# State-space mixer: groups without padding on array halves, a real part in two summands, and the first gated blocks multiplied unsplit inside the loop

## The chip, the cores and the metric

The program runs on one core of a Trainium2 chip. The metric is the device time of one execution in microseconds, the median over runs. One execution was also taken by the hardware profiler; all rows below come from it. Its engines are called PE (TensorE's products), PEld (TensorE's weight loads), DVE (VectorE), ACT (ScalarE), POOL (GpSimd) and SP (SyncE, which here only issues transfers).

## The reference

A small network on 256 tokens of width 1024: six layers, each a mixer and a gated feed-forward block. The change is in the second layer's mixer, a state-space layer (S5) with 64 groups of 16 channels and 64 complex states per group, run forwards and backwards in time:

```python
def _s5_direction(u, lam_re, lam_im, log_dt, b_re, b_im, c_re, c_im, reverse):
    lam_bar = jnp.exp(lam * dt)
    b_bar = ((lam_bar - 1.0) / lam)[..., None] * lax.complex(b_re, b_im)
    bu = einsum('bsgp,gnp->bsgn', u, b_bar)          # complex
    _, hs = lax.associative_scan(combine, (a, bu), axis=1, reverse=reverse)
    return jnp.einsum('gpn,bsgn->bsgp', c, hs).real

def s5_mixer(h, ..., d_skip, w_glu):
    u = h.reshape(b, s, 64, 16)
    y = (y_fwd + y_bwd).reshape(b, s, d) + d_skip * h
    g = jax.nn.gelu(y)
    val, gate = jnp.split(g @ w_glu, 2, axis=-1)      # w_glu: 1024 x 2048
    return val * jax.nn.sigmoid(gate)
```

## The kernel before

Activations lie transposed: 8 channel tiles of 128 partitions by 256 tokens. Time is cut into chunks of L = 4 tokens, so a scan runs over NC = 64 chunk steps. A channel tile kt holds 8 groups, worked on as 4 pairs (pi) of two groups (g2), two directions (d), real and imaginary (i).

Precise products are made by splitting: a weight piece of 1024 columns (half of a 1 MB transfer `raw`, three buffers) is rounded into `whi` on ACT (L134) and the rest subtracted into `wlo` on DVE (L136); an activation is split alike (`split`, L166); three products, hi by hi, lo by hi and hi by lo, replace one float32 product. `piece(n)` (L142) keeps four pieces prepared ahead, and `hold` names the piece ahead of which preparation stops. A product on plain float32 operands appears in the trace as two records for one instruction of the program.

The mixer is `s5` (L1758). `load(kt)` fetches the tables, copies the decay `at` on ACT and scales the inputs by the norm's factor into `u` (L1805), two operations of 64 partitions; u and the output weights `wz` are padded with zeros in the other group's half (memset by POOL, L1793), so that a product of all 128 rows yields one group. `states(kt)`: 32 products into `vp` (PSUM pool `mm`, 4 banks), L1819; four DVE products from PSUM (L1823, L1824, L1826, L1827), a sum and a difference on POOL (L1825, L1828), two DVE scans (L1830, L1831), and the turn back: two products and a sum on POOL (imaginary part, L1834 to L1836), two products and a difference on DVE (real part, L1837 to L1839). `outputs(kt)`: 40 products into one bank `yp` (pool `ms`, 4 banks): a direct term from `mt` (L1849) and four state terms (L1855) for each of eight groups, all in PSUM partitions 0 to 63; a copy `ys` on ACT (L1858), two stores on SP's queue to DRAM (L1860) and one load `g` in another order on ACT's queue (L1862). `gates(kt)`: gelu on ACT (L1867) and the split into `ghi`, `glo`.

The loop (L1877) runs n = 0 to 11: states(n), gates(n - 4), load(n + 1), outputs(n - 2). Behind it, in program order, come the first half of the gated matrix (L1895, pieces 0 to 7 by channel tile, 8 blocks of 128 columns in 4 banks `pf`) and its second half (L1902, pieces 8 to 15, `blockT`), with sigmoid, product and residual per pair of blocks. In front of `s5` stands the first feed-forward block, which stages the mixer's inputs through DRAM (`s5hx`, `s5u`).

The order on each engine's queue is not written out by hand: a planner places every instruction by priority (program order) and its own estimate of when inputs and buffers are ready; the queues then run in that fixed order. `issue_after` adds an order by hand: the first gated pieces may only follow the sixth load of wz (L1888 to L1891).

## Time and profile before

| | us |
|---|---|
| median of 3 runs | 2419.71 |
| lowest and highest run | 2417.47, 2421.77 |
| the profiled execution | 2417.63 |
| its span, first to last instruction | 2415.9 |
| PE busy, share of the span | 2219.3, 92% |
| DVE busy | 1655.8, 69% |
| ACT busy | 1132.0, 47% |
| POOL busy | 628.1, 26% |

Busy is the union of an engine's instructions, its share that of the span. PE's products are pipelined: one record lasts longer than the step to the next, so costs below are read from start to start. A trace can lack a few per cent of its PE records. The mean granted clock of TensorE was 0.953 of full speed.

### The profile page before, as it was taken

The page shows a single profiled execution, that of the slowest core. Times are in us where ns is not written, and L with a number is a line of the kernel's source. Part 1 is how long each engine was busy: PE and PEld are TensorE (multiplying, and loading weights), DVE is VectorE, ACT ScalarE, POOL GpSimd, SP SyncE. Part 2 cuts the span into 40 slices and gives each one's busy share as a digit, 9 for nine tenths or more (in the row PEclk, how much of TensorE's full clock was granted, in tenths as well). Part 3 has the DMA queues.
Part 4 walks back from the last instruction along what each step waited for, and adds up shares of the span by engine and source line. Part 5 has one row for each costly group of instructions (what it writes and reads, how often), then busy time and mean ns, then how long its engine had stood idle before and what let it go on. Part 6 is the DMA issues. An engine that isn't in the chain of part 4 may idle for free.

```text
span 2415.9 us, 45760 instructions
## 1 busy us (share of the span) xinstructions
PE 2219.3 (92%) x19028; PEld 2144.8 (89%) x19028; DVE 1655.8 (69%) x2502; ACT 1132.0 (47%) x2012; POOL 628.1 (26%) x583
## 2 busy tenths in 40 slices
PE   7778786799999996999999999989999999999998
PEld 7777786799999985689999999978899899899998
DVE  7899969776656768356656665874765679467664
ACT  5334321354435565354445444754544565364442
POOL 3986746300013222010011001530200359112001
PEclk9989888999999998999999999999999999799999
DMA  4457666555564432235553554443455333434552
GB/s 167 169 181 247 221 185 168 186 189 180 190 208 153 143 140 86 72 110 184 189 178 106 189 180 174 150 146 106 158 189 180 140 122 123 110 108 148 188 180 104
DMA packets 95117, 383.41 MB, mean 159 GB/s; under 512 B 37132, under 2 KB 44956, under 8 KB 54845
## 3 DMA queue, kind: packets, MB, share of 16 engines
q1 hardware_dynamic: 72400, 359.95, 43.0%
q10 hardware_dynamic: 22508, 20.54, 3.0%
q8 instruction: 149, 2.44, 0.4%
q14 instruction: 60, 0.48, 0.1%
HBM read 361.81 MB, written 18.65 MB: 157 GB/s over the span
## 4 chain that ended last, share of the span: by engine, by line
PE 71%; DVE 15%; POOL 5%; issue 3%; DMA 3%; ACT 3%; ACTq 1%; SPq 0%; POOLq 0%; DVEq 0%
PE pg L162 8%; PE pg L164 8%; PE pg L163 8%; PE po L163 7%; PE po L164 7%; PE po L162 7%; DVE wlo L136 3%; PE f L412 1%; PE pq L162 1%; PE pk L162 1%; PE pq L163 1%; PE pq L164 1%; PE pk L163 1%; PE pk L164 1%; DMA mt<-s5ker 1%
## 5 line engine op out<-in xcount | busy, mean ns | idle before, releaser
L136 DVE TENSOR_TENSOR wlo<-raw,whi 128x1024 fp32r<-128x1024 f32 x623 | 798.7, 1285 | 412.0 <-ACT whi L134 410.7
L134 ACT CAST whi<-raw 128x1024 fp32r<-128x1024 f32 x625 | 651.1, 1047 | 668.0 <-PE pg L163 291.8
L164 PE MATMUL pg<-hhi,wlo 128*128 128x256 f32 x1920 | 545.4, 284 | 24.2 <-DVE wlo L136 24.0
L162 PE MATMUL pg<-hhi,whi 128*128 128x256 f32 x1920 | 544.1, 283 | 6.8 <-ACT whi L134 6.7
L163 PE MATMUL pg<-hlo,whi 128*128 128x256 f32 x1920 | 543.2, 283 | 0.0
L164 PEld LDWEIGHTS pg<-hhi,wlo 128*128 128x128 f32 x1920 | 365.9, 191 | 27.5 <-DVE wlo L136 26.9
L162 PEld LDWEIGHTS pg<-hhi,whi 128*128 128x128 f32 x1920 | 366.2, 191 | 7.5 <-ACT whi L134 7.2
L163 PEld LDWEIGHTS pg<-hlo,whi 128*128 128x128 f32 x1920 | 366.2, 191 | 0.0
L163 PE MATMUL po<-alo,whi 128*128 128x256 f32 x1056 | 299.0, 283 | 1.6 <-DVE alo L171 1.6
L162 PE MATMUL po<-ahi,whi 128*128 128x256 f32 x1056 | 298.0, 283 | 2.2 <-ACT ahi L170 2.2
L164 PE MATMUL po<-ahi,wlo 128*128 128x256 f32 x1056 | 298.9, 283 | 0.0
L226 POOL TENSOR_TENSOR acc<-sq 128x256 f32<-128x256 f32 x16 | 15.7, 983 | 984.4 <-ACT sq L221 984.4
L162 PEld LDWEIGHTS po<-ahi,whi 128*128 128x128 f32 x1056 | 200.2, 190 | 2.4 <-ACT ahi L170 2.4
L163 PEld LDWEIGHTS po<-alo,whi 128*128 128x128 f32 x1056 | 200.5, 190 | 1.8 <-DVE alo L171 1.8
L164 PEld LDWEIGHTS po<-ahi,wlo 128*128 128x128 f32 x1056 | 200.6, 190 | 0.3 <-issue 0.2
L226 POOL TENSOR_TENSOR acc<-acc,sq 128x256 f32<-128x256 f32 x76 | 71.0, 934 | 246.4 <-ACT sq L221 228.9
L313 DVE TENSOR_TENSOR g<-pg,rB 128x512 f32<-128x512 f32 x120 | 82.8, 690 | 30.4 <-PE pg L164 30.4
L170 ACT CAST ahi<-g 128x256 fp32r<-128x256 f32 x132 | 52.5, 400 | 54.8 <-DVE g L316 54.8
L316 DVE TENSOR_TENSOR g<-g 128x256 f32<-128x256 f32 x132 | 71.8, 546 | 8.1 <-ACT g L315 8.1
L315 ACT ACTIVATE g<-g 128x256 f32<-128x256 f32 x132 | 54.2, 413 | 48.4 <-DVE g L313 34.7
L171 DVE TENSOR_TENSOR alo<-g,ahi 128x256 fp32r<-128x256 f32 x132 | 68.0, 517 | 0.0
L163 PE MATMUL pc<-hlo,whi 128*128 128x256 f32 x224 | 65.5, 292 | 0.0
(672 smaller groups left out, 5426.7 us busy)
## 6 DMA issues: line engine op xcount, KB each, us to landing
raw<-in_gu_dram SPq DMA_DIRECT2D x132, 1024.0 KB, 4.9
raw<-in_dn_dram SPq DMA_DIRECT2D x66, 1024.0 KB, 4.8
raw<-in_qkv_dram SPq DMA_DIRECT2D x36, 1024.0 KB, 4.9
raw<-in_hy_in_dram SPq DMA_DIRECT2D x13, 1024.0 KB, 4.9
raw<-in_fnet_dram SPq DMA_DIRECT2D x8, 1024.0 KB, 5.3
raw<-in_s_glu_dram SPq DMA_DIRECT2D x8, 1024.0 KB, 5.1
raw<-in_hy_out_dram SPq DMA_DIRECT2D x8, 1024.0 KB, 4.9
raw<-in_gdn_v_dram SPq DMA_DIRECT2D x8, 1024.0 KB, 4.8
```

The costliest lines, as they stand in the source:

```text
L134: nc.scalar.copy(hi[:, :w], raw[:, s:s + w])
L136: eng.tensor_tensor(lo[:, :w], raw[:, s:s + w], hi[:, :w].bitcast(F32), op=ALU.subtract)
L162: nc.tensor.matmul(ps, whi[:, sl], hi, start=start, stop=False)
L163: nc.tensor.matmul(ps, whi[:, sl], lo, start=False, stop=False)
L164: nc.tensor.matmul(ps, wlo[:, sl], hi, start=False, stop=stop)
L170: nc.scalar.copy(hi, src)
L171: nc.vector.tensor_tensor(lo, src, hi.bitcast(F32), op=ALU.subtract)
L226: nc.gpsimd.tensor_tensor(acc, sums[0], sq, op=ALU.add)
L313: nc.vector.tensor_tensor(gu_, ps, self.rB.unsqueeze(1).to_broadcast([P, 2, T]), op=ALU.mult)
L315: nc.scalar.activation(g, g, AF.Silu)
L316: nc.vector.tensor_tensor(u, u, g, op=ALU.mult)
L412: nc.tensor.matmul(o, a[:, t, c], w[:, r, :], start=n == 0, stop=n == 11)
```

## The change

Four things, all in the state-space mixer and the helper that prepares weight pieces:

- no padding: u is scaled in place (`u0`, one operation of 128 partitions), `wz` has one half less, the memsets of both go, and every product takes only its group's 64 rows, so products lie on quarters of the array (rows by group, columns by group in `states` and by pair in `outputs`). `vp` moves to the pool `ms`; `yp` becomes two banks, `ys` two copies of 128 partitions, and four stores replace two.
- the real part of the states is not subtracted: both summands stay (`s[0]`, `s[1]`) and go into the outputs as two products with the same weights; outputs have 56 products instead of 40.
- the first 8 pieces of the gated matrix are not split (`direct`): the float32 raw weights multiply the float32 gelu output `gf`, one product instead of three, inside the loop, right behind gelu. The splits of `gf` for the second half stand behind the loop.
- `hold` stands behind these 8 pieces, so their transfers may run ahead of the mixer; the order by hand at n == 6 goes.

The optional arguments `full`, `whole` and `hf` are used by no call.

```diff
+        if n in self.direct:
+            self.prep[n] = (raw[:, s:s + w], None)
+            return
...
-            wz = [sp.tile([P, 2, TW], F32, name=f"wz{i}") for i in range(2)]
+            wz = [sp.tile([P, TW], F32, name=f"wz{i}") for i in range(2)]
             def load_w(kt):
-                for g2 in range(2):
-                    r = slice(64 * g2, 64 * g2 + 64)
-                    last = nc.sync.dma_start(wz[kt % 2][r, g2], self.tab[kt, r, :TW])
-                return last.ins
+                nc.sync.dma_start(wz[kt % 2], self.tab[kt, :, :TW])
...
-            for g2 in range(2):
-                r = slice(64 * (1 - g2), 64 * (1 - g2) + 64)
-                for a in u + wz:
-                    nc.gpsimd.memset(a[r, g2], 0.0)
...
-                for g2 in range(2):
-                    r = slice(64 * g2, 64 * g2 + 64)
-                    nc.vector.tensor_tensor(u[kt % 4][r, g2], self.u0[r, 4 * kt:4 * kt + 4, :],
-                                            rc[r].to_broadcast([64, 4, NC]), op=ALU.mult)
+                u = self.u0[:, 4 * kt:4 * kt + 4, :]
+                nc.vector.tensor_tensor(u, u, rc.to_broadcast([P, 4, NC]), op=ALU.mult)
...
             def states(kt, vt, er):
-                vp = [self.mm.tile([P, 512], F32, tag="mm", name="vp") for _ in range(2)]
+                vp = [self.ms.tile([P, 512], F32, tag="ms", name="vp") for _ in range(2)]
-                            for g2 in range(2):
-                                uu = u[kt % 4][:, g2, pi, :] if d == 0 else u[kt % 4][:, g2, pi, ::-1]
+                            for r in (lo, hi):
+                                uu = self.u0[r, 4 * kt + pi, :] if d == 0 else self.u0[r, 4 * kt + pi, ::-1]
-                                nc.tensor.matmul(vp[i][64 * g2:64 * g2 + 64, sg:sg + NC], vt[:, pi, d, i, :], uu,
-                                                 start=True, stop=True)
+                                nc.tensor.matmul(vp[i][r, sg:sg + NC], vt[r, pi, d, i, :], uu, start=True, stop=True)
-                nc.vector.tensor_tensor(t[2], vp[1], er, op=ALU.mult)
-                nc.vector.tensor_tensor(t[3], vp[0], ei, op=ALU.mult)
+                nc.vector.tensor_tensor(t[2], vp[0], ei, op=ALU.mult)
+                nc.vector.tensor_tensor(t[3], vp[1], er, op=ALU.mult)
...
+                s = [x[:, :, 1:] for x in st[kt % 3]]
+                v = [x.rearrange("p (a c) -> p a c", a=8) for x in (*c, er, ei, t[1], t[3])]
+                nc.gpsimd.tensor_tensor(v[4], v[0], v[3], op=ALU.mult)
+                nc.vector.tensor_tensor(s[0], v[0], v[2], op=ALU.mult)
+                nc.gpsimd.tensor_tensor(v[5], v[1], v[2], op=ALU.mult)
+                nc.vector.tensor_tensor(s[1], v[1], v[3], op=ALU.mult)
+                nc.gpsimd.tensor_tensor(s[2], v[4], v[5], op=ALU.subtract)
-                nc.gpsimd.tensor_tensor(t[1], c[0], ei, op=ALU.mult)
-                nc.gpsimd.tensor_tensor(t[3], c[1], er, op=ALU.mult)
-                nc.gpsimd.tensor_tensor(s[1][:, :, 1:], v[1], v[3], op=ALU.add)
-                nc.vector.tensor_tensor(t[0], c[0], er, op=ALU.mult)
-                nc.vector.tensor_tensor(t[2], c[1], ei, op=ALU.mult)
-                nc.vector.tensor_tensor(s[0][:, :, 1:], v[0], v[2], op=ALU.subtract)
...
             def outputs(kt):
-                yp = self.ms.tile([P, 512], F32, tag="ms", name="yp")
-                        nc.tensor.matmul(o, mt[:, 4 * kt + pi, :], u[kt % 4][:, g2, pi, :], start=n == 0, stop=False)
-                                nc.tensor.matmul(o, w5[:, g2, pi, d, i, :], x, start=False, stop=n == 32)
+                yp = [self.ms.tile([P, 512], F32, tag="ms", name="yp") for _ in range(2)]
+                for p2 in range(2):
+                    for n in range(7):
+                        for g2 in range(2):
+                            for ph in range(2):
+                                r, pi = (lo, hi)[g2], 2 * p2 + ph
+                                if n == 0:
+                                    w, x = mt[r, 4 * kt + pi, :], self.u0[r, 4 * kt + pi, :]
+                                else:
+                                    d, i = (n - 1) // 3, (n - 1) % 3
+                                    x = s[i][r, 2 * pi + d]
+                                    x = x[:, 0:NC] if d == 0 else x[:, NC - 1::-1]
+                                    w = w5[r, pi, d, i // 2, :]
+                                nc.tensor.matmul(yp[g2][(lo, hi)[ph], p2 * NC:(p2 + 1) * NC], w, x,
+                                                 start=n == 0 and p2 == 0, stop=n == 6 and p2 == 1)
-                nc.scalar.copy(ys.rearrange("p g a c -> p (g a c)"), yp[0:64, :])
-                for g2 in range(2):
-                    nc.sync.dma_start(yx[kt, :, g2].rearrange("a q i c -> (q i) a c"), ys[:, g2])
+                for g2 in range(2):
+                    nc.scalar.copy(ys[:, g2].rearrange("p a c -> p (a c)"), yp[g2][:, :2 * NC])
+                for ph in range(2):
+                    for g2 in range(2):
+                        nc.sync.dma_start(yx[kt, ph::2, g2].rearrange("a q i c -> (q i) a c"), ys[(lo, hi)[ph], g2])
...
-            def gates(kt, g):
-                h = ss.tile([P, T], F32, tag="h", name="gl")
-                nc.scalar.activation(h.rearrange("p (c i) -> p i c", i=L), g, AF.Gelu_apprx_tanh)
-                self.split(ghi[:, kt, :], glo[:, kt, :], h)
+            first = [self.mm.tile([P, 2, T], F32, tag="mm", name="pf") for _ in range(4)]
+            def gates(k, g):
+                nc.scalar.activation(gf[:, k, :].rearrange("p (c i) -> p i c", i=L), g, AF.Gelu_apprx_tanh)
+                w, _ = self.piece(base + k)
+                for b in range(KD):
+                    nc.tensor.matmul(first[b // 2][:, b % 2], w[:, b * P:(b + 1) * P], gf[:, k, :],
+                                     start=k == 0 and b % 2 == 0, stop=k == KD - 1 and b % 2 == 1)
...
                 if 1 <= n < KD:
-                    last = load_w(n)
-                if n == 6:
-                    self.hold = None
-                    with tc.issue_after(last):
-                        self.piece(base)
+                    load_w(n)
+            for k in range(KD):
+                self.split(ghi[:, k, :], glo[:, k, :], gf[:, k, :])
+            self.hold = None
...
-            first = [self.mm.tile([P, 2, T], F32, tag="mm", name="pf") for _ in range(4)]
-            for k in range(KD):
-                whi, wlo = self.piece(base + k)
-                for b in range(KD):
...
+                    K.direct = {st["s5_glu"] + k for k in range(KD)}
...
-                K.hold = st["s5_glu"]
+                K.hold = st["s5_glu"] + KD
```

## Rows read from the trace of the kernel before

**Rows 1.** Stretches in us: length, busy PE, PEld, DVE, ACT, POOL (records), clock, DMA share, GB/s.

```profile
340.00:348.20 8.20, 8.11 (x69) 7.91 (x67) 0.80 (x3) 0.42 (x1) 0.74 (x1) 1.00 0.00 0
...
371.20:443.80 72.60, 49.02 (x883) 47.85 (x884) 66.99 (x67) 15.44 (x24) 45.00 (x31) 0.83 0.63 184
443.80:457.00 13.20, 9.58 (x104) 9.11 (x102) 13.17 (x10) 2.60 (x4) 6.79 (x4) 0.95 0.42 124
457.00:461.70 4.70, 4.70 (x79) 4.63 (x79) 1.41 (x2) 0.00 (x0) 0.00 (x0) 1.00 0.73 255
461.70:480.00 18.30, 18.03 (x152) 17.83 (x151) 8.72 (x10) 11.29 (x17) 0.00 (x0) 1.00 0.49 174
480.00:502.00 22.00, 21.80 (x192) 21.80 (x193) 19.16 (x29) 14.77 (x27) 5.14 (x6) 1.00 0.53 181
```

**Rows 2.** The chain that ended last, in order of time: start, us, what.

```profile
354.54 21.40 DMA mt<-s5ker
```

**Rows 3.** VectorE in order of time: start, us, line, operation, output<-inputs [idle before].

```profile
360.96 2.27 DVE L1830 TENSOR_TENSOR_SCAN c<-at,t 128x512 f32<-128x512 f32 x1 [0.78 <-POOL t L1825]
363.26 0.69 DVE L1837 TENSOR_TENSOR t<-c,s5ve 128x512 f32<-128x512 f32 x1
363.87 2.29 DVE L1831 TENSOR_TENSOR_SCAN c<-at,t 128x512 f32<-128x512 f32 x1
...
367.52 0.68 DVE L1827 TENSOR_TENSOR t<-vp,er 128x512 f32<-128x512 f32 x1
...
371.15 2.27 DVE L1830 TENSOR_TENSOR_SCAN c<-at,t 128x512 f32<-128x512 f32 x1 [1.15 <-POOL t L1825]
...
400.41 1.23 DVE L1831 TENSOR_TENSOR_SCAN c<-at,t 128x512 f32<-128x512 f32 x1
```

**Rows 4.** GpSimd in order of time, in the loop's first tile.

```profile
368.10 1.27 POOL L1836 TENSOR_TENSOR st<-t,t 128x512 f32<-128x512 f32 x1
```

**Rows 5.** VectorE in order of time: scalings of u, and the last tile's first scan.

```profile
352.38 3.56 DVE L1805 TENSOR_TENSOR u<-s5u,rc 64x256 f32<-64x256 f32 x8 [0.23 <-DVE rc L1781]
...
397.99 0.39 DVE L1805 TENSOR_TENSOR u<-s5u,rc 64x256 f32<-64x256 f32 x1
...
443.80 2.27 DVE L1830 TENSOR_TENSOR_SCAN c<-at,t 128x512 f32<-128x512 f32 x1 [0.80 <-POOL t L1825]
```

**Rows 6.** TensorE in order of time, records merged (xcount), in and behind the mixer.

```profile
354.19 3.67 PE L1819 MATMUL vp<-u,s5ve 128*64 128x64 f32 x60 [0.73 <-DVE u L1805]
...
391.09 2.03 PE L1819 MATMUL vp<-u,s5ve 128*64 128x64 f32 x63
...
418.84 1.11 PE L1855 MATMUL yp<-st,wz 128*64 128x64 f32 x8 [5.12 <-DVE st L1839]
...
1000.47 0.33 PE L735 MATMUL ptb<-ident,p 64*64 64x64 f32 x4
1000.74 0.33 PE L737 MATMUL ptb<-ident,p 128*128 128x128 f32 x1
...
2112.94 0.59 PE L1407 MATMUL sp<-vf,kn 128*128 128x256 f32 x2
2113.37 0.38 PE L1398 MATMUL yp<-vn,ym 128*128 128x128 f32 x2
```

**Rows 7.** Costs by line and shape in 352.4 to 457.0 us: busy, mean ns | idle before.

```profile
L136 DVE TENSOR_TENSOR wlo<-raw,whi 128x1024 fp32r<-128x1024 f32 x4 | 6.9, 1752 | 0.0
```

**Rows 8.** ScalarE in order of time: the first gelu, and the last tile's copy and gelu.

```profile
400.29 0.69 ACT L1867 ACTIVATE gl<-g 128x256 f32<-128x256 f32 x1 [4.93 <-DMA g<-yx]
400.77 0.64 ACT L1858 COPY ys<-yp 64x512 f32<-64x512 f32 x1
...
461.79 0.58 ACT L1858 COPY ys<-yp 64x512 f32<-64x512 f32 x1 [8.66 <-PE yp L1855]
...
470.35 0.66 ACT L1867 ACTIVATE gl<-g 128x256 f32<-128x256 f32 x1 [3.52 <-DMA g<-yx]
```

**Rows 9.** Costs of TensorE by line and shape over the whole span: busy, mean ns.

```profile
L735 PE MATMUL ptb<-ident,p 64*64 64x64 f32 x128 | 11.9, 243 | 0.0
```

More of the change, by code (lines that the diff above doesn't have):

```diff
@@ L69, in __init__ @@
         self.pool_lo = set()
+        self.direct = set()
+        self.hf = None
     def setup(self, rawb=3, prepb=4):
@@ L148, in piece, with blockT, rows, unitT @@
         return self.prep[n]
-    def blockT(self, base, b, KT, hi, lo, ps, u0=None):
-        hi = hi if isinstance(hi, list) else [hi[:, k, :] for k in range(KT)]
-        lo = lo if isinstance(lo, list) else [lo[:, k, :] for k in range(KT)]
+    def blockT(self, base, b, KT, hi, lo, ps, u0=None, full=None):
+        def rows(v):
+            return v if isinstance(v, list) else [v[:, k, :] for k in range(KT)]
+        hi, lo, full = (rows(v) if v is not None else [None] * KT for v in (hi, lo, full))
         for k in range(KT):
-            self.unitT(base, (b * KT if u0 is None else u0) + k, hi[k], lo[k], ps, k == 0, k == KT - 1)
-    def unitT(self, base, u, hi, lo, ps, start, stop):
+            self.unitT(base, (b * KT if u0 is None else u0) + k, hi[k], lo[k], ps, k == 0, k == KT - 1, full[k])
+    def unitT(self, base, u, hi, lo, ps, start, stop, full=None):
         nc = self.nc
@@ L161, in unitT @@
         sl = slice(c, c + P)
+        if wlo is None:
+            nc.tensor.matmul(ps, whi[:, sl], full, start=start, stop=stop)
+            return
         nc.tensor.matmul(ps, whi[:, sl], hi, start=start, stop=False)
@@ L214, in norm_block @@
             self.split(self.hhi[:, k, :], self.hlo[:, k, :], xk, self.gains[:, self.gi, k:k + 1])
+            if self.hf is not None:
+                self.nc.scalar.activation(self.hf[:, k, :], xk, AF.Copy, scale=self.gains[:, self.gi, k:k + 1])
         self.square(self.sums, xk, k == KD - 1)
@@ L292, in sin_turn, with ffn @@
         nc.scalar.activation(out, out, AF.Sin)
-    def ffn(self, gu, dn, next_gi, post=None, full=False, side=(), each=None):
+    def ffn(self, gu, dn, next_gi, post=None, full=False, side=(), each=None, whole=None):
         nc, hp = self.nc, self.hp
         with self.tc.tile_pool(name="ffn", bufs=1, reuse_waits="tile") as fp, self.tc.tile_pool(name="ffs", bufs=2, reuse_waits="tile") as fs:
-            ahi = fp.tile([P, KF, T], F32R, name="ahi")
-            alo = fp.tile([P, KF, T], F32R, name="alo")
+            if whole is None:
+                ahi = fp.tile([P, KF, T], F32R, name="ahi")
+                alo = fp.tile([P, KF, T], F32R, name="alo")
+                af = None
+            else:
+                ahi = alo = None
+                af = fp.tile([P, KF, T], F32, name="af")
             first = [self.mm.tile([P, 2, T], F32, tag="mm", name="pf") for _ in range(2)]
@@ L308, in ffn @@
                     if 2 * j + i >= 3:
-                        self.blockT(gu, 2 * j + i, KD, self.hhi, self.hlo, ps[:, i])
+                        self.blockT(gu, 2 * j + i, KD, self.hhi, self.hlo, ps[:, i], full=whole)
                 if j == 0:
@@ L315, in ffn, with out_proj @@
                 nc.scalar.activation(g, g, AF.Silu)
-                nc.vector.tensor_tensor(u, u, g, op=ALU.mult)
-                self.split(ahi[:, j, :], alo[:, j, :], u)
+                if whole is None:
+                    nc.vector.tensor_tensor(u, u, g, op=ALU.mult)
+                    self.split(ahi[:, j, :], alo[:, j, :], u)
+                else:
+                    nc.vector.tensor_tensor(af[:, j, :], u, g, op=ALU.mult)
             for _ in side:
                 pass
-            self.out_proj(dn, KF, ahi, alo, next_gi, post, lambda: fp.tile([P, KD, T], F32, name="m"), full, each)
-    def out_proj(self, base, KT, hi, lo, next_gi, post=None, mtile=None, full=False, each=None, nk=0):
+            self.out_proj(dn, KF, ahi, alo, next_gi, post, lambda: fp.tile([P, KD, T], F32, name="m"), full, each, whole=af)
+    def out_proj(self, base, KT, hi, lo, next_gi, post=None, mtile=None, full=False, each=None, nk=0, whole=None):
         nc, hp = self.nc, self.hp
@@ L339, in out_proj @@
                 ps = self.mm.tile([P, 512], F32, tag="mm", name="po")[:, :T]
-                self.blockT(base, b, KT, hi, lo, ps)
+                self.blockT(base, b, KT, hi, lo, ps, full=whole)
             if post is None:
@@ L1782, in s5 @@
             at = [sp.tile([P, 8, NC], F32, name=f"at{i}") for i in range(2)]
[L1783 to L1785 removed]
+            st = [[sp.tile([P, 8, NC + 1], F32, name=f"st{i}{j}") for j in range(3)] for i in range(3)]
             mt = sp.tile([P, NP, 64], F32, name="mt")
             yx = sd.tile([KD, 4, 2, 16, L, NC], F32, name="yx")
+            gf = sp.tile([P, KD, T], F32, name="gf")
             ghi = sp.tile([P, KD, T], F32R, name="ghi")
             glo = sp.tile([P, KD, T], F32R, name="glo")
[L1790 to L1793 removed]
             for a in at + st[0] + st[1] + st[2]:
                 nc.gpsimd.memset(a[:, :, 0:1], 0.0)
+            lo, hi = slice(0, 64), slice(64, P)
             def load(kt):
```

23 lines of the change are left out of this document (4 added, 19 removed).

## The prediction

> **What bounds the kernel now.** I first read the granted clock and the busy time of each engine over the whole span: TensorE is at work nearly all the time, so only a stretch where it waits can give much back. Then I cut the mixer's stretch, from the last product of the block before it (348.1 us) to the first product of the block behind it (502.1 us), into pieces with the view of stretches [rows 1]; the two ends are read from TensorE's order of time. The reader is to see two regimes. From 371.2 to 457.0 us VectorE is busy 92 to 100% of the time and TensorE 68 to 73%, at a clock of 0.83 to 0.95: the loop over the eight channel tiles is set by VectorE. From 457.0 to 502.1 us TensorE is busy without a gap: it does the last tile's outputs (4.7 us), catches up on the first half of the gated blocks (18.3 us) and does the second half (22.0 us).
>
> Inside the loop I read the order of time on VectorE and GpSimd [rows 3, 4]. The same scan takes 2.29 us beside a GpSimd operation and 1.23 us beside none, while an operation that reads PSUM keeps its 0.68 us beside one. So operations of VectorE with both inputs in SBUF take turns with GpSimd's, and the loop's period is the sum of the two engines' such operations, not the larger one. Per tile that is five GpSimd operations of about 1.27, two scans of about 1.2 and three SBUF products or sums of 0.6 (the row of 363.26: the next operation starts 0.61 later): 10.5, and the first period, which has nothing else in it, was 371.15 - 360.96 = 10.2 us [rows 3]. The four products from PSUM hide under GpSimd. The mean of the seven periods is (443.80 - 360.96)/7 = 11.8 [rows 3, 5]: two scalings of u, a subtraction for glo, and one wait on TensorE, which itself sat behind the load of mt until 376 us [rows 2].
>
> **The change, part by part.** I sum against the profiled execution's own 2417.63 us.
>
> Start. Eight scalings of u take 3.56 us ahead of the first product, GpSimd clears padding meanwhile; afterwards one scaling of 0.39 does [rows 5]. The first states then start about 1.0 earlier (their 64 records keep the low clock, 3.7 us [rows 6]), and since both products of the first sum now come first, GpSimd starts 0.6 earlier. -1.6 (bounds 0 and -3.2, all of the scalings).
>
> Period. Removed per tile: one SBUF subtraction (0.6), one of two scalings, the subtraction for glo. GpSimd's count stays five. From 10.2 I take off 0.6 and put on 0.6 for one scaling, its 0.39 and some blocking: 10.2 again, but now in all seven periods. 7 x (11.8 - 10.2) = -11.4. Bounds: 9.4 if every lock is packed (-17), 11.8 if the new order of the queues gives nothing (0). The mt wait should go: yp and vp now share four PSUM slots, which leaves little room for outputs of later tiles ahead of vp; if it stays, about 2 us of the 11.4 are lost.
>
> End of the loop. The last tile takes 13.2 us from its scan to 456.9, in which four weight splits take 6.9 [rows 5, 7]. Without them 6.2, without the subtraction 5.6. The eight first pieces are no longer split. Pieces 8 to 11 still are, as soon as their transfers land, and nothing holds them behind the loop: I put two at 1.5 into it. 8.6: -4.6 (bounds -7.6 for none, -1.6 for four).
>
> TensorE under the loop. A record of 64 columns takes 0.059 us where all outputs lie in one half of the columns (79 records in 4.70, [rows 1]) and 0.029 where two halves take turns (63 in 2.03 less the last one's 0.22, [rows 6]). Afterwards states are 64 records as now, outputs 112 instead of 80 (seven terms instead of five, no padding). At 0.029 these are 1.9 and 3.3 us. An unsplit product of 256 columns has no row here with these operands; the nearest, L1407, takes 0.43 us for its two records until the next product starts [rows 6]; eight per tile make 3.4. Sum 8.6 per tile, under a period of 10.2: hidden. Bounds: outputs 1.65 with four quarters at a time, 6.6 with none together (states then 3.7, sum 13.7: TensorE sets the period). I take 0.029, as two records of one product must still follow each other in one quarter. Turning between quarters and the whole array costs too: four records of 64x64 take 0.33 us in all and 0.24 for one [rows 6, 9], so they start 0.03 apart, but the whole-array record behind them starts 0.27 after the first, where 0.12 would do. Two turns of 0.15 per tile: 8.9, so 1.3 us of cover are left, where it had 11.8 - 1.9 - 4.7 = 5.2.
>
> The Trainium skill (TensorEngine Tiling (Array Packing), Restrictions and Gotchas) says that different row tiles cannot write one PSUM bank at the same time. The states' two row halves do share a bank here, so by that rule they would take 3.7 and not 1.9, TensorE 10.7 per tile, and the four iterations that hold all three kinds 0.5 each, some 2 us in all. The row of L735 speaks against it: its products alternate over both diagonal quarters of one bank and start 0.03 us apart [rows 6, 9].
>
> Behind the loop. Now: 457.0 to 502.1, 45.1 us. Afterwards 64 unsplit products replace 192 split ones, all but the last eight under the loop, and the last tile's way through memory, which the catch-up hid, lies bare. Outputs 3.3; copies, four instead of two stores on SP's queue (half the size each, taken as equal in sum), the load on ScalarE's queue and gelu: 461.79 to 470.35 + 0.66, 9.2 us [rows 8]; the last eight products 3.4; low clock, 2.5 (bounds 0 and 3.4), since TensorE has idled about 9.2 - 3.4 = 5.8 us by then, and after an idle of 5.12 eight of its records took 1.11 [rows 6], where seven steps of 0.059 and the last one's 0.22 make 0.63; the second half, the release of its first bank in it, 22.0 as now [rows 1]. Together 40.4: -4.7. The eight late splits of gf, each a quarter of a weight split in columns, and the splits of pieces 8 to 11 lie in the 9.2, where ScalarE and VectorE have little else; without that cover they would cost VectorE 8 x 0.44 + 4 x 1.75 = 10.5 [rows 7].
>
> Weights. Three transfers of the gated weights now precede the loop; in 340 to 348 us the DMA engines stand still [rows 1], so I cost them at nothing; they stand on SP's queue ahead of s5hx, which waits for later data anyway. The next ones wait for the products of tiles 1, 3 and 5; each can hold SP's queue, behind which the tables of the next tile stand.
>
> Sum: -1.6 - 11.4 - 4.6 - 4.7 = -22.3, so 2395.3 for the execution. The profiled execution stands 2.1 below the median of the three runs (2419.71), so I predict 2395.3 + 2.1 = 2397.
>
> **Rivals.** (B) TensorE takes the cover away. The products on gf stand in TensorE's order, and each waits for a transfer; vp of a next tile stands behind it. Or the quarters don't overlap, and four periods grow from 10.2 to 13.7. Either way the periods' 11.4 are gone: 2409. For it: a cover of only 1.3 us per tile, and gelu already waiting 4.93 us for its transfer [rows 8]. Against: vp is wanted some 7 us after its slots come free.
>
> (C) Slower. In ScalarE's queue the first gelu stood ahead of the second tile's ys and held it [rows 8]. If that order is kept for every tile and the products on gf go ahead of the next outputs, a tile becomes a ring: outputs 3.3, round trip 9.2, products 3.4, 15.9 us instead of 10.2. Seven times 5.7 is 40: 2437. It decides from a period of 10.2 + 22.3/7 = 13.4 on. Against: in the later tiles of before ys did not wait for gelu, and two iterations lie between outputs and gates in the program.
>
> (D) Within noise: the same stalls, only in part, a period of about 13.
>
> (E) Better: the locks pack (9.4), no split falls into the loop, the clock holds: 2397 - 5.6 - 3.0 - 2.5 = 2386.
>
> **How the numbers follow.** 0.2% of 2420 is 4.8 us, about what a measurement can tell from no change. Forecast 0.50, E 0.08, B 0.25, D 0.07, C 0.10. Faster by over 0.2% are the first three, 0.83; within 0.2% D, 0.07; slower C, 0.10. For 8 in 10 the range takes in E and B with some 4 us beyond B for the loss of the start's gain and the mt wait: 2385 to 2413. Predicted 2397.
>
> **What would show it.** Right: scans of successive tiles 9.5 to 10.5 us apart; the loop's last sum near 439 instead of 456.9; outputs at 0.029 per record; about 9 us between the last ys and the last products, with only one earlier group of products in it; the block behind starting near 480. Wrong: TensorE waiting for gelu in the middle of the loop with vp behind it; VectorE idle until vp; weight splits between the scans. The forecast falls if the periods stay at 11.8 or the splits of pieces 8 to 11 come behind the last products.

## The result, and the profile after

| kernel | runs | median, us | lowest, highest |
|---|---|---|---|
| before | 4 | 2419.19 | 2417.47, 2421.77 |
| changed | 4 | 2441.35 | 2435.41, 2448.07 |

The changed kernel takes 1.0085 times as long as the one before, with an interval of 1.0061 to 1.0109; a second comparison, beside the last experiments, gave 1.0085 again (1.0057 to 1.0113). Forecast were 2397 us and a gain. The profiled execution took 2448.07 us, its span 2446.3.

Two lengths are compared below. One is the median. The other is the mixer in the trace, from the end of the last product of the block before it to the first product of the block behind it: 153.96 us before (348.11 to 502.07), 173.73 after (349.34 to 523.07). The rest of the program executes the same instructions in every kernel here, yet took between 2256 and 2278 us from profile to profile (last section), so a single execution says less of the mixer than its own length does.

The mixer's length falls into three parts. From its start to the first scan: 12.85 before, 11.88 after. From the first scan of the first tile to that of the last: 82.84 before [rows 3, 5], 101.14 after. From there to the next block: 58.27 before, 60.71 after. So nearly all of the loss is in the loop, in the very part for which most of the gain was forecast. The changed kernel by stretches answers to [rows 1] (the columns are the same):

```profile
371.20:465.00 93.80, 52.86 (x1082) 45.16 (x1077) 49.16 (x55) 11.32 (x26) 44.77 (x32) 0.78 0.42 128
465.00:499.80 34.80, 19.24 (x235) 15.41 (x226) 13.09 (x15) 11.52 (x23) 5.39 (x3) 0.75 0.36 115
499.80:523.00 23.20, 23.20 (x194) 23.16 (x193) 17.06 (x24) 12.77 (x23) 5.10 (x6) 1.00 0.48 167
```

VectorE, busy 92 to 100% of the loop before, is busy 49.16 of 93.80 us now, and no engine has taken its place: TensorE has 52.86. Everybody waits. The view of waits in 350 to 505 us (the wait; us in total, times, longest) says for whom:

```profile
DVE glo L180 <- ACT ghi L179: 54.9, 6, 11.6
ACT gf L1887 <- DMA g<-yx: 52.0, 7, 12.6
...
PE pf L1890 <- ACT gf L1887: 40.7, 6, 9.0
ACT at L1816 <- DVE c L1844: 31.6, 5, 9.0
```

The first line is the new one; four of its six waits lie in the loop. `glo` is the subtraction of the late splits, which stand behind the loop in the program. In the kernel before, the first such subtraction in the loop stood behind both scans of its tile and waited for nothing (VectorE, right behind the last of [rows 3]):

```profile
401.74 1.54 DVE L171 TENSOR_TENSOR glo<-gl,ghi 128x256 fp32r<-128x256 f32 x1
```

VectorE of the changed kernel in order of time, in the third and fourth tile, answers to [rows 3]:

```profile
380.36 2.27 DVE L1842 TENSOR_TENSOR_SCAN c<-at,t 128x512 f32<-128x512 f32 x1 [1.33 <-POOL t L1837]
...
388.00 0.68 DVE L1839 TENSOR_TENSOR t<-vp,er 128x512 f32<-128x512 f32 x1
398.08 0.43 DVE L180 TENSOR_TENSOR glo<-gf,ghi 128x256 fp32r<-128x256 f32 x1 [9.41 <-ACT ghi L179]
398.43 1.22 DVE L1842 TENSOR_TENSOR_SCAN c<-at,t 128x512 f32<-128x512 f32 x1
...
402.61 0.69 DVE L1850 TENSOR_TENSOR st<-c,er 128x512 f32<-128x512 f32 x1
...
416.95 0.43 DVE L180 TENSOR_TENSOR glo<-gf,ghi 128x256 fp32r<-128x256 f32 x1 [11.26 <-ACT ghi L179]
417.29 1.22 DVE L1842 TENSOR_TENSOR_SCAN c<-at,t 128x512 f32<-128x512 f32 x1
```

The first scans of the eight tiles start at 361.22, 370.69, 380.36, 398.43, 417.29, 436.46, 453.55 and 462.36. Two periods are 9.5 and 9.7 us, better than the 10.2 forecast. Then the planner has put the subtraction of tile k straight ahead of the first scan of tile k + 3 (tiles counted from 0), and four periods are 18.1, 18.9, 19.2 and 17.1. ScalarE in the same time shows the other half of a ring; it answers to [rows 8]:

```profile
385.64 0.61 ACT L1816 COPY at<-s5am 128x504 f32<-128x504 f32 x1 [9.04 <-DVE c L1844]
386.16 0.42 ACT L1875 COPY ys<-yp 128x128 f32<-128x128 f32 x2
394.16 0.33 ACTq L1880 DMA_DIRECT2D g<-yx  x1
...
396.96 0.65 ACT L1887 ACTIVATE gf<-g 128x256 f32<-128x256 f32 x1 [1.17 <-DMA g<-yx]
397.65 0.40 ACT L179 CAST ghi<-gf 128x256 fp32r<-128x256 f32 x1
402.61 0.61 ACT L1816 COPY at<-s5am 128x504 f32<-128x504 f32 x1 [4.55 <-DVE c L1844]
403.12 0.42 ACT L1875 COPY ys<-yp 128x128 f32<-128x128 f32 x2
413.75 0.33 ACTq L1880 DMA_DIRECT2D g<-yx  x1
415.83 0.65 ACT L1887 ACTIVATE gf<-g 128x256 f32<-128x256 f32 x1 [12.28 <-DMA g<-yx]
```

Read it as one turn: copy `ys` at 386.16, through memory, gelu at 396.96, rounding `ghi` at 397.65, subtraction on VectorE at 398.08, two scans, and only when the second scan ends (402.61) may ScalarE's copy of the decay `at` go, behind which the next `ys` stands (403.12). A turn takes 10.8 us through memory and 6.2 on the engines, 17.0; the next one 12.7 and 6.2. The last turn is short, because no decay is left to copy and no table to fetch: `ys` stands right behind `ghi` (453.08), its trip to gelu takes 6.2 us, the subtraction of tile 4 waits for nothing, and the last period is 8.8.

Other rows answer as follows. The wait for `mt` [rows 2] is gone from TensorE (its output products start at 369.73 us, where before all but four records waited until 376.08). All eight scalings of u stand in one row of VectorE, 2.77 us (before, eight of the sixteen took 3.56 [rows 5]); TensorE does not wait for the end of this row, its states start at 354.45, 0.53 us behind the row's start.

### The profile page after: what moved, and what is told of

It is laid out like the page before. It is cut to its first block, busy times and chain, and to the rows that moved or that the text cites. A ratio compares the mean times of both kernels' runs of the same rounds, so it can differ in the third digit from the quotient of the medians.

```text
span 2446.3 us, 46117 instructions
## 1 busy us (share of the span) xinstructions
PE 2224.9 (91%) x19220; PEld 2141.5 (88%) x19220; DVE 1617.4 (66%) x2478; ACT 1123.2 (46%) x2012; POOL 623.9 (26%) x574
## 4 chain that ended last, share of the span: by engine, by line
PE 71%; DVE 13%; POOL 6%; issue 3%; ACT 3%; DMA 3%; SPq 0%; ACTq 0%; POOLq 0%; DVEq 0%
PE pg L173 8%; PE pg L171 8%; PE pg L172 8%; PE po L172 7%; PE po L171 7%; PE po L173 7%; DVE wlo L141 3%; PE f L432 1%; PE pq L171 1%; PE pk L171 1%; PE pq L172 1%; PE pq L173 1%; PE pk L172 1%; PE pk L173 1%; PE pv L627 1%
## 5 line engine op out<-in xcount | busy, mean ns | idle before, releaser
L141 DVE TENSOR_TENSOR wlo<-raw,whi 128x1024 fp32r<-128x1024 f32 x615 | 788.8, 1286 | 424.3 <-ACT whi L139 421.9
L139 ACT CAST whi<-raw 128x1024 fp32r<-128x1024 f32 x617 | 642.8, 1048 | 667.9 <-PE pg L172 297.5
L173 PE MATMUL pg<-hhi,wlo 128*128 128x256 f32 x1920 | 546.1, 284 | 15.9 <-DVE wlo L141 15.7
L173 PEld LDWEIGHTS pg<-hhi,wlo 128*128 128x128 f32 x1920 | 367.0, 191 | 18.7 <-DVE wlo L141 18.3
L1890 PE MATMUL pf<-gf,raw 128*128 128x256 f32 x128 | 42.6, 505 | 40.7 <-ACT gf L1887 40.7
L1890 PEld LDWEIGHTS pf<-gf,raw 128*128 128x128 f32 x128 | 32.7, 262 | 48.6 <-ACT gf L1887 41.8
L334 DVE TENSOR_TENSOR g<-g 128x256 f32<-128x256 f32 x132 | 65.8, 500 | 8.1 <-ACT g L332 8.1
```

The costliest lines, as they stand in the source:

```text
L139: nc.scalar.copy(hi[:, :w], raw[:, s:s + w])
L141: eng.tensor_tensor(lo[:, :w], raw[:, s:s + w], hi[:, :w].bitcast(F32), op=ALU.subtract)
L173: nc.tensor.matmul(ps, wlo[:, sl], hi, start=False, stop=stop)
L334: nc.vector.tensor_tensor(u, u, g, op=ALU.mult)
L1890: nc.tensor.matmul(first[b // 2][:, b % 2], w[:, b * P:(b + 1) * P], gf[:, k, :], start=k == 0 and b % 2 == 0, stop=k == KD - 1 and b % 2 ...
```

## The experiments

Three theories stood at the beginning. Theory 1: the ring just read. Theory 2, my rival B: the products on gelu's output in TensorE's order hold states and outputs. Theory 3: the small products or the doubled stores cost more than they save. Each ratio below is to the kernel before, executed beside the run, with its 95% interval; the mixer is its length in the run's trace, in us.

**The packing alone.** The kernel has no padding and the real part in two summands; the gated blocks stay as in the kernel before.

```diff
-                nc.scalar.activation(gf[:, k, :].rearrange("p (c i) -> p i c", i=L), g, AF.Gelu_apprx_tanh)
-                w, _ = self.piece(base + k)
-                for b in range(KD):
-                    nc.tensor.matmul(first[b // 2][:, b % 2], w[:, b * P:(b + 1) * P], gf[:, k, :],
-                                     start=k == 0 and b % 2 == 0, stop=k == KD - 1 and b % 2 == 1)
+                h = ss.tile([P, T], F32, tag="h", name="gl")
+                nc.scalar.activation(h.rearrange("p (c i) -> p i c", i=L), g, AF.Gelu_apprx_tanh)
+                self.split(ghi[:, k, :], glo[:, k, :], h)
```

> The unpadded groups on array halves and the real part as two summands alone; the gated blocks stay as in the kernel before (all 16 pieces split, products behind the loop, splits of gelu's output in the loop). Theory 1 (the loss is a ring from the outputs' copy through memory to gelu, its subtraction on VectorE, the scans, the copy of the decay and the next outputs' copy): two iterations lie between outputs and gates here too, but nothing on TensorE waits for gelu, so I expect the period to fall from 11.8 to about 9.7 us if the subtractions do not stand ahead of a scan that waits; 7 x 2.1 = 14.7 off, the last tile's outputs 1.9 instead of 4.7, start nothing: about 2400, 2395 to 2412. Theory 2 (the products on gelu's output in TensorE's order hold the states) says the same here. Theory 3 (the small products or the four stores themselves cost the time): 2425 or more.

Measured: 2444.88 us, ratio 1.0085 (1.0065 to 1.0104), mixer 179.47. Against theory 1's number, but not against its mechanism: the condition that I had attached (no subtraction ahead of a scan that waits) does not hold. Its view of waits begins like that of the changed kernel:

```profile
DVE glo L180 <- ACT ghi L179: 52.1, 7, 10.2
ACT gl L1885 <- DMA g<-yx: 52.0, 7, 12.4
```

Here the splits stand in the loop in the program, and the planner put four of them ahead of the scans too (why it did so here and not in the kernel before is not recorded); the scans of tiles 2 to 6 are 16.5 to 17.8 us apart. So theory 2 is not needed for the loss, since no product in this loop reads gelu's output. Theory 3 gave the right time here and falls with the next run.

**The late subtractions.** The changed kernel, with one order by hand:

```diff
-                nc.vector.tensor_tensor(s[1], v[1], v[3], op=ALU.mult)
+                self.last_dve = nc.vector.tensor_tensor(s[1], v[1], v[3], op=ALU.mult)
...
-            for k in range(KD):
-                self.split(ghi[:, k, :], glo[:, k, :], gf[:, k, :])
+            with tc.issue_after(self.last_dve.ins):
+                for k in range(KD):
+                    self.split(ghi[:, k, :], glo[:, k, :], gf[:, k, :])
```

> The changed kernel, with VectorE's subtractions of the late splits put behind its last product of the last tile's states; ScalarE's part of the splits and all else as it is. Theory 1: the ring loses its way through VectorE, but ScalarE still copies outputs k+1 behind gelu k, so one round trip through memory of about 12.3 us per tile stays: scans then 9.6 to 12.5 us apart instead of 17 to 19, last gelu near 466 us instead of 494, total about 2416 to 2422. Theory 2 (TensorE's order: products on gelu's output ahead of the next states and outputs): the periods stay near 18, 2435 or more. Theory 3: 2435 or more.

Measured: 2415.93 us, ratio 0.9961 (0.9940 to 0.9982), mixer 145.78, 27.95 less than in the changed kernel. The last gelu came at 467.25. The scans of tiles 1 to 6 follow at 9.5 to 9.7 us (one row of VectorE for each end of this stretch, and the one late scan behind it):

```profile
370.56 2.28 DVE L1842 TENSOR_TENSOR_SCAN c<-at,t 128x512 f32<-128x512 f32 x1 [1.19 <-POOL t L1837]
...
418.89 2.27 DVE L1842 TENSOR_TENSOR_SCAN c<-at,t 128x512 f32<-128x512 f32 x1 [1.32 <-POOL t L1837]
...
434.20 2.27 DVE L1842 TENSOR_TENSOR_SCAN c<-at,t 128x512 f32<-128x512 f32 x1 [0.78 <-POOL t L1837]
```

Theory 1 holds, theories 2 and 3 fall as causes of the loss: the same products, stores and TensorE order are in this kernel. From the mixer's start to the next block, the traces of this run and of the changed kernel show the same instructions in the same order on VectorE, ScalarE, GpSimd and SyncE's queue, but for five subtractions that moved behind the last tile's states. On ScalarE one round trip per tile is left (gelu at 395.77, 407.02, 419.98, each behind the last).

**Which second link closes the ring?** The subtraction ahead of a scan costs a delay once; it makes a loss in each turn only if the next outputs wait for that scan. First the decay copies were given four buffers, the subtractions left alone:

```diff
-            at = [sp.tile([P, 8, NC], F32, name=f"at{i}") for i in range(2)]
+            at = [sp.tile([P, 8, NC], F32, name=f"at{i}") for i in range(4)]
```

> The changed kernel with four buffers instead of two for the copied decay, so that these copies on ScalarE wait for no late scan; the subtractions of the late splits stay where they are, ahead of the scans. Theory 1: the ring needs both VectorE's subtraction ahead of the scans and ScalarE's copy of the decay behind them; with the copy gone, the next outputs' copy follows gelu directly, and the ring is the round trip of 12.3 us alone: periods 12 to 13.5, total 2415 to 2425. If the subtraction alone is to blame (VectorE waiting for each transfer, whatever stands on ScalarE), the periods stay 17 to 19 and the total 2435 to 2448. Theory 2: 2435 or more.

Measured: 2440.95 us, ratio 1.0063 (1.0040 to 1.0086), mixer 172.30, periods 17.8, 17.3, 20.6, 17.2. Theory 1's number is missed. SyncE's queue in order of time shows why: the fetch of the next table of turning factors waits for VectorE's last product of the tile and stands ahead of the four stores.

```profile
419.05 0.33 SPq L1776 DMA_DIRECT2D s5ve<-s5rt  x1
419.47 0.38 SPq L1786 DMA_DIRECT2D wz<-s5tab  x1
419.94 4.17 SPq L1878 DMA_DIRECT2D yx<-ys  x4
```

The first of these rows is a table fetch of the next tile (`er` or its other buffer `s5ve`). For what it waits, the view of waits of SyncE's queue in 350 to 505 us tells:

```profile
SPq L1776 <- DVE st L1850: 51.6, 6, 12.2
```

`ys` was copied at 412.55 and left only at 419.94. So the ring has two second links, side by side. The next run took both away: four buffers, and the stores on ScalarE's own queue.

```diff
-                        nc.sync.dma_start(yx[kt, ph::2, g2].rearrange("a q i c -> (q i) a c"), ys[(lo, hi)[ph], g2])
+                        nc.scalar.dma_start(yx[kt, ph::2, g2].rearrange("a q i c -> (q i) a c"), ys[(lo, hi)[ph], g2])
```

> The run with four buffers for the copied decay, and the four stores of each tile issued by ScalarE right behind the copy instead of by SyncE; the subtractions stay ahead of the scans. In the run with four buffers alone the periods stayed at 17 to 20 us, and SyncE's queue shows the fetch of the next decay table, which waits for VectorE's last state product, ahead of the stores. Theory: that fetch closed the ring in the place of the copy; without both, the next outputs leave right behind gelu and the round trip alone sets the period, 10.5 to 13 us, total 2410 to 2424. Rival (VectorE's wait for each transfer is the whole of it, no ring): periods 17 or more, 2433 or more.

Measured: 2431.50 us, ratio 1.0040 (1.0024 to 1.0056), mixer 161.81. VectorE's first waits stay (9.95 and 8.31 us; periods 18.6, then 15.9 with one copy of the decay that still waits); the last three periods are 8.8, 11.1 and 12.9, where the run before had 20.6, 17.2 and 8.8. The ring is open from there on, as expected. The total lies above what I gave and below the rival's 2433: the first delay is not a matter of the ring, and from the last scan to the next block it takes 63.9 us (446.48 to 510.42), in which ScalarE waits 12.3 for weights.

The reverse was tried on the kernel before, where ScalarE has the next outputs' copy right behind gelu:

```diff
+                if 3 <= n <= 6:
+                    gates(n - 3, ys.pop(n - 3))
                 if n < KD:
                     states(n, *tabs.pop(n))
-                if n >= 4:
+                if n >= 8:
                     gates(n - 4, ys.pop(n - 4))
...
-                nc.vector.tensor_tensor_scan(c[0], a, t[0], 0.0, op0=ALU.mult, op1=ALU.add)
+                with tc.issue_after(self.last_lo.ins):
+                    nc.vector.tensor_tensor_scan(c[0], a, t[0], 0.0, op0=ALU.mult, op1=ALU.add)
```

The order by hand is for tiles 3 to 6 alone, `last_lo` is the last subtraction of `split`.

> The kernel before with nothing of the change, but with the split of gelu's output of tiles 0 to 3 put ahead of the first scan of tiles 3 to 6, where the planner put it in the changed kernel; its own place there was behind the second scan of the same tile. Theory 1: the same ring closes in the old kernel, four periods of 16 to 19 us instead of 12, so 15 to 28 us more: 2435 to 2450. Rival (the ring needs the shorter loop, the four stores or the products on gelu's output as well): 2416 to 2428.

Measured: 2419.28 us, ratio 1.0000 (0.9979 to 1.0022), mixer 153.43. My number was wrong, the rival's right. The subtraction does stand ahead of the scan and waits, but little (VectorE in order of time):

```profile
401.92 0.43 DVE L171 TENSOR_TENSOR glo<-gl,ghi 128x256 fp32r<-128x256 f32 x1 [2.71 <-ACT ghi L170]
402.26 1.22 DVE L1832 TENSOR_TENSOR_SCAN c<-at,t 128x512 f32<-128x512 f32 x1
...
410.37 0.42 DVE L171 TENSOR_TENSOR glo<-gl,ghi 128x256 fp32r<-128x256 f32 x1 [0.50 <-ACT ghi L170]
```

On ScalarE the next `ys` follows gelu directly (400.51 and 400.97, 409.23 and 410.25), ahead of the copy of the decay. Its stores leave at once (401.62, 410.85), ahead of the table's fetch (405.45, 416.93), and the trips behind the first take 7.6 to 9.4 us, less than the loop's own 11.8. This fits a ring of two links: a VectorE instruction that waits for memory ahead of the scans, and outputs that wait for those scans. But this run does not separate the missing second link from the longer period, which by itself covers such trips. That the second link is needed rests on the run with the stores on ScalarE's queue and on the last turn of the changed kernel.

**Two tiles on their way at once** (the run named apart). To the late subtractions an order on ScalarE was added: gelu of tile k behind the copy of outputs k + 1.

```diff
+                with tc.issue_after(self.last_ys.ins):
+                    nc.scalar.activation(gf[:, k, :].rearrange("p (c i) -> p i c", i=L), g, AF.Gelu_apprx_tanh)
-                nc.scalar.activation(gf[:, k, :].rearrange("p (c i) -> p i c", i=L), g, AF.Gelu_apprx_tanh)
```

> As the run with the late subtractions, and gelu k also stands behind the copy of outputs k+1 on ScalarE, so that two tiles can be on their way through memory at once. Theory 1: no ring of less than two tiles is left, scans 9.5 to 10 us apart in all seven periods, last gelu near 449 us, 20 us less than in the run with the late subtractions alone in the loop's tail: about 2396 to 2405. Theory 2: as without it, 2435 or more.

Measured: 2419.88 us, ratio 0.9975 (0.9958 to 0.9992), mixer 144.83, last gelu 465.90: less than 1 us of the 20 forecast. The medians (2415.93 and 2419.88) do not even stand in the order of the mixers; the intervals of the two ratios overlap, so no difference of time between these runs is shown. Scans were 9.5 to 9.7 apart but for tiles 5 (11.2) and 7 (13.6), counted from 0. Towards the end ScalarE itself waits, for weights, ahead of outputs that were done at about 434 us (ScalarE in order of time):

```profile
437.97 1.99 ACT L139 CAST whi<-raw 128x1024 fp32r<-128x1024 f32 x2 [9.35 <-DMA raw<-in_s_glu_dram]
439.87 0.42 ACT L1875 COPY ys<-yp 128x128 f32<-128x128 f32 x2
```

**The weight splits behind the loop as well** (the run named latecast).

```diff
+            while self.n_raw <= self.pieces[base + KD][0] + self.rawb - 1:
+                self._emit_raw(self.n_raw)
+                self.n_raw += 1
+            with tc.issue_after(self.last_ys.ins):
+                self.piece(base + KD)
```

> The run named apart, and the splits of the gated pieces 8 to 11 also stand behind the last copy of outputs on ScalarE (their transfers stay where they were). In the run named apart ScalarE stood idle ahead of the copies of tiles 4 to 7 behind a rounding that waited for its weights: outputs of tile 4 were done near 434 us and copied at 439.9. Theory: these roundings are the second kind of wait that the planner put into the loop; without them the last four tiles follow at 9.7 to 12 us, last gelu near 453 instead of 466 us, the mixer 144.8 us becomes 132 to 137, total 8 to 12 us below the run named apart, about 2407 to 2412. Rival (the round trips through memory are bound by the transfers or by TensorE's products at half clock, not by ScalarE's order): last gelu 462 to 467, mixer 143 to 147, no gain.

Measured: 2408.28 us, ratio 0.9944 (0.9926 to 0.9963), mixer 141.89, last gelu 462.57. The median is where the theory put it, the mixer is not (132 to 137); by the trace the rival is nearer. What holds the last tile's states is TensorE's order, rival B after all, in a small way; its products for tile 7 start at 428.85, behind a wait for gelu, and VectorE waits 4.64 us for them (TensorE, then VectorE in order of time):

```profile
421.30 5.94 PE L1891 MATMUL pf<-gf,raw 128*128 128x256 f32 x16 [6.59 <-ACT gf L1888]
427.17 0.34 PE L1870 MATMUL yp<-s5u,mt 64*64 64x64 f32 x8
...
428.85 2.05 PE L1832 MATMUL vp<-s5u,vt 64*64 64x64 f32 x64
```

```profile
430.82 0.69 DVE L1835 TENSOR_TENSOR t<-vp,er 128x512 f32<-128x512 f32 x1 [4.64 <-PE vp L1832]
```

**The products one iteration later.**

```diff
-            for n in range(KD + 4):
+            for n in range(KD + 5):
...
+                if n >= 5:
+                    products(n - 5)
```

`products` holds the eight products that `gates` held, ordered by hand behind the last product of outputs n - 2.

> The run named latecast, and the products on gelu's output of tile k come one iteration later on TensorE, behind the outputs of tile k + 3, so that no states and no outputs stand behind a product that waits for gelu. In the run named latecast the scans of tiles 5 and 7 still came 1.4 and 4.2 us late, behind states that stood behind such products, and outputs of tiles 5 to 7 waited in the same way. Theory 2, my rival B, as a remainder: with these gone all seven periods are 9.6 to 9.8 us, the last scan starts near 429 instead of 434 us, the last gelu near 448 to 454 instead of 462.6, and the mixer falls from 142 to 126 to 135 us: total 2391 to 2403. Rival (the round trips themselves set the last tiles, whatever TensorE's order): scans 9.7 us apart, but the last gelu stays at 460 us or more, total 2405 to 2412.

Measured: 2400.56 us, ratio 0.9915 (0.9893 to 0.9938), mixer 134.22, last gelu 447.73. Theory 2 holds as this remainder. All seven periods are 9.5 to 9.7 us (first scan 359.45, last 426.99; VectorE in order of time, the last three):

```profile
407.62 2.27 DVE L1842 TENSOR_TENSOR_SCAN c<-at,t 128x512 f32<-128x512 f32 x1 [1.35 <-POOL t L1837]
...
417.30 2.27 DVE L1842 TENSOR_TENSOR_SCAN c<-at,t 128x512 f32<-128x512 f32 x1 [1.35 <-POOL t L1837]
...
426.99 2.27 DVE L1842 TENSOR_TENSOR_SCAN c<-at,t 128x512 f32<-128x512 f32 x1 [1.36 <-POOL t L1837]
```

This version, the change with four orders by hand (late subtractions, gelu behind the next copy, late weight splits, late products), is faster than both kernels. What is left behind its loop is one more wait of ScalarE for weights, ahead of the first sigmoid, for which TensorE waits 5.03 us (ScalarE in order of time):

```profile
453.58 1.99 ACT L139 CAST whi<-raw 128x1024 fp32r<-128x1024 f32 x2 [4.73 <-DMA raw<-in_s_glu_dram]
455.59 1.28 ACT L1932 ACT_TABLE_LOAD   x1
456.88 0.66 ACT L1932 ACTIVATE sg<-pf 128x256 f32<-128x256 f32 x2
```

**The packing with a late subtraction.** The packing alone, its split of tile k ordered behind the states of tile k + 4:

```diff
+                with tc.issue_after(self.last_dve.ins):
+                    self.split(ghi[:, k, :], glo[:, k, :], h)
-                self.split(ghi[:, k, :], glo[:, k, :], h)
```

> The run of the packing alone, with the split of gelu's output of tile k put behind VectorE's last state product of tile k + 4 instead of ahead of the scans of tile k + 3. Theory 1 (that one subtraction makes the loss): scans 9.6 to 9.8 us apart throughout, mixer 136 to 144 us instead of 154.0 in the kernel before, total 2405 to 2413. Rival (unpadded products, two summands and four stores cost about what they save): 2417 or more.

Measured: 2418.77 us, ratio 0.9995 (0.9982 to 1.0008), mixer 157.61. The mixer is 21.9 us shorter than with the packing alone, and the scans are 9.5 to 10.5 us apart (359.42 to 429.44 for all eight), 12.8 us less than in the kernel before. But the time is that of the kernel before, and the mixer 3.65 longer: the last tile and what stands behind it wait for what the shorter loop no longer covers. VectorE has a weight split ahead of the last tile's second scan, TensorE waits for outputs to be copied and for a table (VectorE, then TensorE in order of time).

```profile
437.44 1.23 DVE L141 TENSOR_TENSOR wlo<-raw,whi 128x1024 fp32r<-128x1024 f32 x1 [5.72 <-ACT whi L139]
...
440.32 1.22 DVE L1843 TENSOR_TENSOR_SCAN c<-at,t 128x512 f32<-128x512 f32 x1
```

```profile
442.40 0.64 PE L1869 MATMUL yp<-s5u,mt 64*64 64x64 f32 x8 [9.16 <-ACT ys L1874]
447.15 1.56 PE L1869 MATMUL yp<-st,wz 64*64 64x64 f32 x48 [4.11 <-DMA wz<-s5tab]
```

Both come from ScalarE's roundings, which wait 8.59 us for their weights up to 436.36, ahead of the copies: TensorE's first wait directly, its second because the table's fetch (440.85) stands on SyncE's queue behind four weight transfers (430.54 to 440.76), which wait for the splits to free their buffers. I expected a gain of 7 us or more; the loop's was given back whole, to the same kind of wait in another place.

## Why the prediction was wrong, point by point

**The step that failed** is the sentence that the eight late splits of gf "lie in the 9.2, where ScalarE and VectorE have little else". I priced them at what they cost as work (0.4 us each) in the place where the program has them. The kernel's order is the planner's: it put five of them ahead of scans, and four of these waited there for a transfer, 9.41, 11.26, 11.56 and 9.48 us, 41.7 us of waiting for 1.7 us of work. In the sum it is the term of the period that failed: it took "the subtraction for glo" out of the loop and gave -11.4, measured were +18.3 (82.84 to 101.14). The 10.2 us of a period counted only instructions, and there was no term for an instruction that waits in VectorE's queue. The sign follows from this alone: with the subtractions late the mixer is 27.95 us shorter, and faster than before.

**The argument against rival C** failed with it. Its price (15.9 us per tile, 2437) was near what came (17 to 19, 2441), its way only in part: the order on ScalarE that it named, gelu ahead of the next `ys`, is in the ring, but it ran through the products on gf, and the packing alone has the ring without them. "Two iterations lie between outputs and gates" is no protection, since the way from the states' scan through outputs, copy and memory to gelu and back is as long as the iterations between; and what closed the ring, the copy of the decay and the table's fetch ahead of the stores, I had not looked at, though [rows 8] shows gelu and copies in one queue.

**The period's other terms** were right, and a little low in gain: 9.5 to 9.7 us where nothing waits, forecast 10.2 with 9.4 as the bound; the 0.6 put on for a scaling is not in the loop, since all eight stand ahead of it. Over seven periods that is 15.3 us (82.84 against 67.54 in the run with the late products), forecast 11.4.

**Start**: forecast 1.6, measured 1.0 (12.85 to 11.88). The 1.0 of the states came: the bulk of them starts 5.11 us behind the block before, where it was 6.08. The scalings were not what held them: [rows 5, 6] show TensorE at work from 354.19, before the row of eight ends (355.94). The 0.6 from GpSimd did not come: the planner ran VectorE's four products in the order L1835, L1838, L1836, L1839, so the first sum still waits for the third. **The wait for mt** went, as forecast.

**TensorE under the loop**: states at 0.029 us per record as forecast (64 in 2.05 less the last one's 0.22). Outputs were cheaper: 112 records in 1.68 (427.17 to the next product at 428.85 in the run with the late weight splits), 0.015 each, a quarter of 0.059. Four quarters work at once, and I had taken the step of two, since two records of one product must follow each other; that did not hold the four quarters up. Eight unsplit products take 3.65 from start to start at full clock (3.4 forecast), 3.72 with the last one's end, but 5.4 to 6.3 behind a wait (in the changed kernel 6.31 at 397.67, at a granted clock of 0.58 of the full 2.4 GHz, part of it at the lower level). The Trainium skill (TensorEngine Tiling (Array Packing), Restrictions and Gotchas) says that different row tiles cannot access one PSUM bank at the same time. The states' 0.029 does not bear this out for these products, whose row halves share a bank but not its partitions.

**Rival B** was real, but cost 8 us of the mixer (141.89 to 134.22) and not the whole gain.

**End of the loop and behind it**: forecast 9.3 off. In the run with the late products the stretch from the last scan to the next block is 55.26 against 58.27, 3.0 off. The outputs end 7.9 earlier after the scan (10.02 against 17.95; forecast 6.0), but from there to the second half it takes 20.8 us, where I had 9.2 + 3.4 + 2.5: the copy waits behind a load in ScalarE's queue, and the second half for the sigmoid; the second half itself takes 24.5, not 22.0. The splits of pieces 8 to 11, priced as work at 1.5 us each, are here too a wait: 4.73 us of ScalarE ahead of the sigmoid, and 9.35 us ahead of a copy of outputs in the run named apart. In the changed kernel this part came as forecast: 35.8 us from the end of the outputs to the next block, forecast 37.1.

**The sum**: in the run with the late products start, loop and end are 1.4, 15.3 and 3.0 off, 19.7 in the mixer against a forecast of 22.3, and the median is 2400.56 against 2397. That this comes near the forecast is in part luck: the loop gave 3.9 more than its term, the end 6.3 less. And it is another kernel than the planned one, with four orders by hand that the prediction did not have.

## What to carry to other kernels

An instruction that waits for a trip through memory is priced by what stands behind it in its engine's queue, not by its own time: before pricing work as hidden, ask who decides its place and whether the estimate behind that place knows the length of the trip (10.8 to 13.0 us in the four long turns of the changed kernel, where the planner put the subtraction 9.4 to 11.6 us too early; what it reckoned with is not on record). Then look for the way back: such a wait costs once, unless something that feeds the next trip stands behind it on any queue, a store behind a fetch included, and then it costs in every turn. And a gain in a loop must be followed to the stage behind it: the packing saved 12.8 us of loop and not a microsecond of time.

## What the runs showed of the hardware

The four quarters of the array together took records of 64 columns at 0.015 us each, two diagonal quarters at 0.029. In the kernel before, with all 128 rows, it was 0.029 where two halves of the columns take turns and 0.059 in one half; one quarter alone was not measured.

Four stores of one tile take SyncE's queue 2.5 to 4.2 us, against 1.23 to 1.60 for two in the kernel before; a trip through memory, from the outputs' copy to gelu, took 6.9 us at the end of the changed kernel's loop (487.23 to 494.08); inside it 10.8 to 13.0 in the four long turns and 6.2 in the fifth, where the stores left at once.

The rest of the program, with the same instructions, took 2256.2 us in one profile of the changed kernel (its second) and 2278.2 in that of the experiment on the kernel before. The clock differs. In the last layer, 2050 to 2140 us, the granted clock was 0.83 and 0.75 of full speed in these two (us, PE busy, clock, DMA share, GB/s):

```profile
2050.00:2140.00 90.00, 82.91 (x875) 0.83 0.38 117
```

```profile
2050.00:2140.00 90.00, 85.20 (x834) 0.75 0.39 111
```

What decides how long the lower level (1.2 GHz) lasts there was not tried. Single executions of one kernel lie up to 21 us apart (2412.57 to 2433.59 for the one before), so a gain of 4 us in the mixer needs the trace to be seen.
